# Two PSUM banks for the projections in the whole kernel, and another order of the fp32 matmuls in each block

## Chip, core and metric

One core of a Trainium2 chip runs the whole kernel. The metric is the device time of one execution in microseconds, given as the median of several runs; the profile is one further execution of the same program, taken by the hardware profiler. Its engines are TensorE (PE, matmuls and transpositions; PEld is its weight load), VectorE (DVE), ScalarE (ACT), GpSimd (POOL), and SyncE (SP), which issues most DMAs. Matmul results land in PSUM, which this kernel uses as eight banks of 128 partitions x 512 fp32.

## What is computed

One layer of a hybrid trunk, for 256 prompt tokens and 8 x 16 sample tokens, that is T = 384 columns. All matrices are fp32.

```python
u = rmsnorm(x)                                  # D_MODEL = 2048
proj = u @ w_in                                 # columns: pool | z | xBC | dt | gates
# branch A: windowed means (2, 4, 8, 16) minus self, a map per group of channels
d = win / cnt - p;  a_pool = (d @ pool_w[g]) * pool_scale
# branch B: causal convolution and silu on x, B, C, then a chunked scan with a state
dt = softplus(dt_raw + dt_bias);  cum = cumsum(dt * A)
cb = einsum('btgn,bsgn->btsg', C, B)
y = einsum('btsgr,bsgrp->btgrp', cb * exp(cum_t - cum_s), x * dt)    # within a chunk
y = y + einsum('btgn,bgrpn->btgrp', C, h) * exp(cum)                 # from the state
h = h * exp(last) + einsum('bsgn,bsgr,bsgrp->bgrpn', B, w_end, x * dt)
a_ssd = gated_rmsnorm(y + d_skip * x, z)
m = sigmoid(gA) * (a_pool @ w_pool_proj) + sigmoid(gB) * (a_ssd @ w_ssd_proj)
x = x + rmsnorm(m @ w_out)
x = x + rmsnorm(relu(rmsnorm(x) @ w_up) ** 2 @ w_down)
```

The outputs are x of both groups of requests, and the new pooling, convolution and scan states.

## The kernel before

**A projection.** Most of the work is `out[128, 384] = W.T @ x`, with the tokens as columns. To keep fp32 accuracy in the fp32r format, both sides are split into a high and a low part, and each product is three matmuls (`mm3`, lines 81 to 83: high x high, high x low, low x high). Weights come in units of 128 x 1024, which hold 8 contraction tiles: SP loads a unit (`wfetch`, tag w, three buffers), ACT rounds its high part (line 72), DVE subtracts (line 74, `wl`); the high and low parts have three buffers each. A projection of 2048 inputs is two units ("halves"), 48 matmuls; `w_ssd` has four. Each projection is one PSUM tile `pj_...`, which one DVE instruction (two for the pooling) reads when it is done.

**PSUM.** There are two pools. `psm` has two banks (`mmtile`), `pss` has six (`sstile`), and each new tile of a pool takes its banks in turn, so that its first write waits until the tile that held the bank before has been read. `bank[0]` says which pool `proj` takes. It is `sstile` everywhere but in the loop over blocks, where it is `mmtile`; everything else (transpositions, norms, the scan's tiles, the outputs of w_out and w_down) is in `sstile` throughout.

**Order.** Instructions are recorded in program order with the tiles that they read and write; a scheduler then sets the order on each engine, each of which runs its instructions strictly in that order. `behind` (line 59) ties an instruction behind another; in the blocks, `half` and `lump` use it to chain projections and groups of small matmuls on TensorE as they are written.

**The stages,** with their time in the profile:

1. To some 36 us: x is loaded and split, pj_p0 and pj_p1 (early, in `sstile` by name) and pj_p2 are computed, and the norm of x (`norm_bc`, bc_x, line 109) gives `rstd`.
2. To 190 us: `pool_tile` (line 223) for 16 tiles, four of each window. It reads `pj_p` with rstd into one of two buffers `pbuf` (lines 230 and 231), fills in the state (line 237), forms the window sums `win` (line 246), the difference `d` (lines 249 to 262) and its split `dh`, `dl` (lines 265, 266). `pool_map` (line 269) multiplies four of these with `pool_w` into `pw` tiles.
3. `dt_phase` (line 295): pj_dt, then a chain of some twenty DVE instructions on 64 partitions (lines 303 to 319) that ends in `cum`, the exponentials, `dtw`, and eleven small transpositions `tk` (line 345) to `tok`. Then, to some 470 us, 16 times a gate projection `pj_ga` (read by `gat`, line 290) and a `pj_pp` (read by `ma`, line 363).
4. To some 1300 us: eight blocks (line 646). In each, six projections `pj_x` through the convolution (`conv`), four `pj_z`, most often a `pj_gb`, and the scan for two pairs of heads. The scan's fp32 matmuls stand in two lumps: after the fifth `pj_x` (trB, yT, Y, pp, cb, trx, yi) and after the last `pj_z` (yT, Y, pp, trx, yi). trB and trx are transpositions of B and x (three records for each 128 x 384), yT puts the transposed state term into the two Y tiles and Y adds to it with 64-column tiles (`128*64`), cb is C times B, yi is C times the state with 32-column tiles (`128*32`) into one half of a bank `py`, and pp is the new state of the prompt into the other half. fp32 matmuls other than transpositions show as two records each. After them, `bside` reads trB, `mside` makes `cbm` from cb on DVE (line 525), `final` reads Y and pp, `xside` reads trx and yi, and `eside` forms the decay `E` with exponentials on ACT.
5. To 1780 us: the last gates, `pj_sp` (w_ssd), and w_out with the tokens as rows (`moving`).
6. From 1780 us: x1 = x + norm (line 849), 16 tiles `trm` of three transpositions each (line 859) with their split x1h, x1l (lines 863, 864), the norm of x1 by way of `dg` (line 879) and bc2 (line 881) to r2, then eight rounds of eight `pj_up` (read with r2, line 903) and the products with w_down (`wd`, three banks at a time).

Of the kernel before, what the change touches and what calls it, by code (L numbers as in the profile page):

```python
# [15 lines left out]
T = 384  # L16
# [18 lines left out]
def build(ctx, tc, io):  # L35
# [15 lines left out]
    def mmtile(name):  # L51
        return psm.tile([P, 512], F32, tag="mm", name=name)

    def sstile(name):
        return pss.tile([P, 512], F32, tag="ss", name=name)
# [27 lines left out]
        return te.matmul(out, wl, xh, start=False, stop=last)  # L83

    last = [None]
    bank = [sstile]
    chain = [False]

    def half(o, q, wl_, rhs):
# [276 lines left out]
    with tc.tile_pool(name="phd", bufs=2, reuse_waits="tile") as pd, tc.tile_pool(  # L366
# [46 lines left out]
        def lump(fn):  # L413
            with behind(last[0]):
                last[0] = fn()
# [15 lines left out]
        def t_trB(D):  # L431
            D.tr = sstile(f"trB{D.g}")
            for b in range(3):
                i = te.transpose(D.tr[:, b * P : b * P + P], D.BT[:, b * P : b * P + P], ident)
            return i
# [204 lines left out]
            S.h0 = S.qd * 4  # L640
            return S

        bank[0] = mmtile
        chain[0] = True
        prev = None
        for g in range(G + 1):
            if g == G:
                dside(prev.p[1])
                gate_b()
                state(prev.p[1])  # L650
                gate_b()
                py = sstile("pp_last")
                lump(lambda: t_yT(prev.p[1]))
                lump(lambda: t_Y(prev.p[1]))
                lump(lambda: t_pp(prev.p[1], py))
                final(prev.p[1])
                gate_b()
                gate_b()
                finish(prev)
                break  # L660
            u0 = 49 + g * 10
            D = Pair()
            D.g = g
            D.p = [pair(D, jp) for jp in range(2)]
            D.xs, D.zs = [], []
            D.BT = conv(u0, 32 + g, "BT", 2)
            pload(D.p[0])
            if g:
                dside(prev.p[1])
            D.CT = conv(u0 + 1, 40 + g, "CT", 2)  # L670
            if g:
                state(prev.p[1])
            D.xs.append(conv(u0 + 2, g * 4, "xs", 6))
            cload(D.p[0])
            cside(D)
            D.xs.append(conv(u0 + 3, g * 4 + 1, "xs", 6))
            D.xs.append(conv(u0 + 4, g * 4 + 2, "xs", 6))
            S = D.p[0]
            lump(lambda: t_trB(D))
            bside(D)  # L680
            if g:
                lump(lambda: t_yT(prev.p[1]))
                lump(lambda: t_Y(prev.p[1]))
            S.py = sstile(f"py{S.nm}")
            if g:
                lump(lambda: t_pp(prev.p[1], S.py))
            lump(lambda: t_cb(D))
            lump(lambda: t_trx(S))
            lump(lambda: t_yi(S))
            if g:  # L690
                final(prev.p[1])
            xside(S)
            mside(D)
            D.xs.append(conv(u0 + 5, g * 4 + 3, "xs", 6))
            eside(S, 0)

            def zproj(j):
                ps = proj(in_units(u0 + 6 + j), xg, f"z{g}_{j}")
                z = pd.tile([P, T], F32, tag="zs", name=f"zs{g}_{j}", bufs=7)
                v.tensor_tensor(z, ps, rstd, ALU.mult)  # L700
                s.activation(z, z, AF.Silu)
                D.zs.append(z)

            zproj(0)
            if g:
                finish(prev)
            pload(D.p[1])
            eside(S, 1)
            zproj(1)
            dside(S)  # L710
            zproj(2)
            state(S)
            cload(D.p[1])
            zproj(3)
            S1 = D.p[1]
            lump(lambda: t_yT(S))
            lump(lambda: t_Y(S))
            S1.py = sstile(f"py{S1.nm}")
            lump(lambda: t_pp(S, S1.py))
            lump(lambda: t_trx(S1))  # L720
            lump(lambda: t_yi(S1))
            final(S)
            xside(S1)
            if g < NG:
                gate_b()
            eside(S1, 0)
            eside(S1, 1)
            prev = D
        bank[0] = sstile
        while gates:  # L730
            gate_b()
        chain[0] = False
# [135 lines left out]
    with tc.tile_pool(name="phg", bufs=1, reuse_waits="tile") as pg, tc.tile_pool(  # L868
        name="phg2", bufs=2, reuse_waits="tile"
    ) as pg2:  # L870
        st = pg.tile([P, 3, 4], F32, name="st2")
        for b in range(3):
            for i in range(4):
                q = pg2.tile([P, 512], F32, tag="q3", name=f"q2_{b}_{i}")
                s.activation(q, x1[:, b, blk(i)], AF.Square, accum_out=st[:, b, i : i + 1])
        dg = pg.tile([P, 3, P], F32, name="dg2")
        for b in range(3):
            y = postnorm(pg2, st, b, "n2")
            v.tensor_scalar(dg[:, b, :], ident, y, None, ALU.mult)
        bc = sstile("bc2")  # L880
        te.matmul(bc[:, :T], ones, dg.rearrange("p b t -> p (b t)"), start=True, stop=True)  # L881
        s.copy(r2, bc[:, :T])
        hacc = pg.tile([P, 3, DM], F32, name="hacc")
        gpo = pg.tile([P, DM], F32, name="gpo2")
        gp.dma_start(gpo, io["g_mlp_post"].partition_broadcast(P))
        s.activation(gpo, gpo, AF.Copy, scale=-0.5)
        st3 = pg.tile([P, 3, 4], F32, name="st3")
        pg.tile([P, 96], F32, name="pad_e")
        NC = 8
        for c8 in range(NC):  # L890
            hh = []
            for f8 in range(8):
                f = c8 * 8 + f8
                if f == 0:
                    ps = sstile("pj_up0")[:, :T]
                    half(ps, 0, wload(io["w_up"][0, 0], "up0_0"), xs2)
                    hold[:] = gate
                    half(ps, 1, wload(io["w_up"][0, 1], "up0_1"), xs2)
                else:
                    ps = proj([io["w_up"][f, 0], io["w_up"][f, 1]], xs2, f"up{f}")  # L900
                    hold[:] = [None, None]
                t = pg2.tile([P, T], F32, tag="t", name=f"ht{f}")
                v.scalar_tensor_tensor(out=t, in0=ps, scalar=0.0, in1=r2, op0=ALU.max, op1=ALU.mult)
                s.activation(t, t, AF.Square)
                h = pg2.tile([P, T], F32R, tag=f"hh{f8}", name=f"hh{f}", bufs=1)
                l = pg2.tile([P, T], F32R, tag=f"hl{f8}", name=f"hl{f}", bufs=1)
                s.activation(h, t, AF.Copy)
                v.tensor_tensor(l, t, h.bitcast(F32), ALU.subtract)
                hh.append((h, l))
            for nb in range(4):  # L910
                o = [sstile(f"wd{c8}_{nb}_{b}") for b in range(3)]

                def done(b):
                    dst = hacc[:, b, blk(nb)]
                    if c8 == 0:
                        s.copy(dst, o[b])
                        return
                    v.tensor_tensor(dst, o[b], dst, ALU.add)  # L918
                    if c8 < NC - 1:
                        return  # L920
                    q = pg2.tile([P, 512], F32, tag="q3", name=f"q3_{nb}_{b}")
                    s.activation(q, dst, AF.Square, accum_out=st3[:, b, nb : nb + 1])  # L922
                    if nb < 3:
                        v.tensor_tensor(dst, dst, gpo[:, blk(nb)], ALU.mult)
                        return
                    if b == 0:
                        pg.tile([P, 32], F32, name="pad_z")
                    z3 = pg.tile([P, 512], F32, name=f"z3_{b}")
                    v.tensor_tensor(z3, dst, gpo[:, blk(nb)], ALU.mult)
                    y = postnorm(pg2, st3, b, "n3", doubled=True)  # L930
                    for i in range(4):
                        z = z3 if i == 3 else hacc[:, b, blk(i)]
                        v.scalar_tensor_tensor(  # L933
                            out=z, in0=z, scalar=y, in1=x1[:, b, blk(i)], op0=ALU.mult, op1=ALU.add
                        )
                        sy.dma_start(io["y"][b][:, blk(i)], z)

                moving(
                    o,
                    [(io["w_down"][c8, nb, kp], f"wd{c8}_{nb}_{kp}") for kp in range(4)],  # L940
                    hh,
                    4 if c8 == NC - 1 and nb == 3 else 0,
                    done,
                    pg,
                )
# [116 lines left out]
```

## Time and profile before

| what | us |
|---|---|
| median of 3 runs | 2871.39 (2870.82 to 2871.83) |
| the profiled execution | 2871.82 |
| its span, first to last instruction | 2870.1 |
| TensorE waits behind pj_dt, at tk | 15.1 and 1.2 |
| TensorE waits at bc2, behind the last trm | 10.3 |
| TensorE waits at the first pw | 1.4 |
| mean granted TensorE clock in the span | 0.993 |

How to read it: TensorE is in use for nearly the whole span, while DVE is idle for nearly half of it and ACT for more, so time in which TensorE waits or runs at a lower clock counts in full, and idle time of the others counts only where TensorE waits for them. Matmuls overlap in their records: one of 384 columns is shown with 0.33 us, but the next starts 0.17 us after it; so distances between starts are to be read, not lengths. "PEclk" is the share of full clock that TensorE was granted, in tenths, in each of 40 slices of the span. A row of the time line gives the start and the length in us, engine, line, operation, out<-in tiles, the array's tile (rows*columns) and the operand's shape, the number of records merged, and in brackets the engine's idle time before it with the instruction that ended it.

### The profile page before, as it was taken

Reading aid. Unit: us, or ns where it says so; the run is one execution under the profiler, and the core shown is the slowest. Engines: PE = TensorE matmul, PEld = TensorE weight load, DVE = VectorE, ACT = ScalarE, POOL = GpSimd, SP = SyncE. Lnnn points to the kernel's source line nnn. Section 1 sums busy time; section 2 is a strip of 40 time slices with the busy share of each in tenths; the row PEclk is TensorE's granted clock in tenths of the full one; section 3 lists DMA queues with packets and bytes.
Section 4 is the critical chain, followed back from the end, with each engine's and each line's share of the span. In section 5 each row is a group of like instructions: output and inputs, shape, how many; then the busy total and the mean of one; then the engine's idle time right before and its main releaser. Section 6 shows DMA issues by size and latency. Waiting matters only on the chain. (4 is left out here: it accounts for less than half of the span.)

```text
span 2870.1 us, 39341 instructions
## 1 busy us (share of the span) xinstructions
PE 2824.9 (98%) x15823; PEld 2680.8 (93%) x15823; DVE 1568.9 (55%) x2251; ACT 1095.1 (38%) x1590; POOL 96.5 (3%) x156
## 2 busy tenths in 40 slices
PE   9979999999999999999999999899999999999998
PEld 8979999999999999999999987889898999989897
DVE  7773334677876886877533335434444444444445
ACT  5432224354544554444422234433232333333233
POOL 0000000000100100101000000000000000000000
PEclk9989999999999999999999999999999999999999
DMA  6433445556555655566644453334444343334433
GB/s 208 139 111 124 139 143 192 171 186 211 191 183 208 201 181 202 195 210 210 205 153 150 147 183 117 110 126 130 126 127 130 125 132 125 129 128 126 132 125 125
DMA packets 141654, 448.77 MB, mean 156 GB/s; under 512 B 17200, under 2 KB 40816, under 8 KB 136864
## 3 DMA queue, kind: packets, MB, share of 16 engines
q1 hardware_dynamic: 133152, 410.14, 43.9%
q0 software_dynamic: 8320, 36.13, 3.5%
q8 instruction: 124, 2.03, 0.3%
q14 instruction: 58, 0.48, 0.1%
HBM read 404.48 MB, written 41.72 MB: 155 GB/s over the span
## 5 line engine op out<-in xcount | busy, mean ns | idle before, releaser
L81 PE MATMUL pj_up<-x1h,wh_up 128*128 128x384 f32 x1024 | 343.4, 335 | 0.0
L82 PE MATMUL pj_up<-x1l,wh_up 128*128 128x384 f32 x1024 | 342.7, 335 | 0.0
L83 PE MATMUL pj_up<-x1h,wl_up 128*128 128x384 f32 x1024 | 342.7, 335 | 0.0
L74 DVE TENSOR_TENSOR wl_wd<-w_wd,wh_wd 128x1024 fp32r<-128x1024 f32 x127 | 155.6, 1225 | 262.0 <-ACT wh_wd L72 262.0
L777 PE MATMUL wd<-wl_wd,hh 128*128 128x512 f32 x762 | 296.7, 389 | 0.0
L778 PE MATMUL wd<-wh_wd,hl 128*128 128x512 f32 x762 | 296.6, 389 | 0.0
L776 PE MATMUL wd<-wh_wd,hh 128*128 128x512 f32 x762 | 296.2, 389 | 0.0
L74 DVE TENSOR_TENSOR wl_up<-w_up,wh_up 128x1024 fp32r<-128x1024 f32 x128 | 156.9, 1226 | 208.9 <-ACT wh_up L72 208.9
L72 ACT ACTIVATE wh_wd<-w_wd 128x1024 fp32r<-128x1024 f32 x127 | 135.0, 1063 | 350.4 <-PE wd L778 282.6
L72 ACT ACTIVATE wh_up<-w_up 128x1024 fp32r<-128x1024 f32 x128 | 136.0, 1064 | 336.3 <-PE pj_up L82 275.7
L81 PE MATMUL pj_x<-xgh,wh_x 128*128 128x384 f32 x768 | 257.5, 335 | 0.0
L83 PE MATMUL pj_x<-xgh,wl_x 128*128 128x384 f32 x768 | 256.6, 334 | 0.0
L82 PE MATMUL pj_x<-xgl,wh_x 128*128 128x384 f32 x768 | 256.6, 334 | 0.0
L81 PEld LDWEIGHTS pj_up<-x1h,wh_up 128*128 128x128 f32 x1024 | 192.8, 188 | 0.6 <-issue 0.3
L82 PEld LDWEIGHTS pj_up<-x1l,wh_up 128*128 128x128 f32 x1024 | 192.8, 188 | 0.6 <-issue 0.3
L83 PEld LDWEIGHTS pj_up<-x1h,wl_up 128*128 128x128 f32 x1024 | 192.7, 188 | 0.0
L81 PE MATMUL pj_z<-xgh,wh_z 128*128 128x384 f32 x512 | 171.1, 334 | 0.0
L83 PE MATMUL pj_z<-xgh,wl_z 128*128 128x384 f32 x512 | 171.1, 334 | 0.0
L82 PE MATMUL pj_z<-xgl,wh_z 128*128 128x384 f32 x512 | 171.0, 334 | 0.0
L81 PE MATMUL pj_sp<-abh,wh_sp 128*128 128x384 f32 x512 | 171.0, 334 | 0.0
L82 PE MATMUL pj_sp<-abl,wh_sp 128*128 128x384 f32 x512 | 171.0, 334 | 0.0
L83 PE MATMUL pj_sp<-abh,wl_sp 128*128 128x384 f32 x512 | 171.0, 334 | 0.0
(291 smaller groups left out, 6058.4 us busy)
## 6 DMA issues: line engine op xcount, KB each, us to landing
w_up<-w_up SPq DMA_DIRECT2D x128, 512.0 KB, 3.4
w_wd<-w_down SPq DMA_DIRECT2D x128, 512.0 KB, 3.4
w_x<-w_in SPq DMA_DIRECT2D x96, 512.0 KB, 4.2
w_z<-w_in SPq DMA_DIRECT2D x64, 512.0 KB, 3.5
w_sp<-w_ssd SPq DMA_DIRECT2D x64, 512.0 KB, 3.5
w_ga<-w_in SPq DMA_DIRECT2D x32, 512.0 KB, 3.4
w_pp<-w_pp SPq DMA_DIRECT2D x32, 512.0 KB, 3.4
hs<-ssm SPq DMA_DIRECT2D x16, 1024.0 KB, 6.0
```

The lines of the kernel that those rows point to most:

```text
L72: s.activation(h, w, AF.Copy)
L74: v.tensor_tensor(l, w, h.bitcast(F32), ALU.subtract)
L81: te.matmul(out, wh, xh, start=first, stop=False)
L82: te.matmul(out, wh, xl, start=False, stop=False)
L83: return te.matmul(out, wl, xh, start=False, stop=last)
L776: te.matmul(o[b], mh, wh[:, c], start=k == 0, stop=False)
L777: te.matmul(o[b], mh, wl[:, c], start=False, stop=False)
L778: te.matmul(o[b], ml, wh[:, c], start=False, stop=k == nk - 1)
```

## The change

`bank` starts as `mmtile` and is never set again, so every projection of `proj` is in the two banks of `psm`, in all stages; pj_up0, which is written out by hand, also goes there, while pj_p0 and pj_p1 stay in `sstile`. So in stages 1 to 3, 5 and 6, the six banks hold only the other tiles. In the blocks, the lumps are written in another order. First lump: cb, trB, trx, yT, Y, yi, pp in place of trB, yT, Y, pp, cb, trx, yi, with `mside` right behind cb in place of behind `xside`. Second lump: trx, yT, Y, yi, pp in place of yT, Y, pp, trx, yi. As `py` is now taken last in the first lump, it takes the bank that cb had.

```diff
     last = [None]
-    bank = [sstile]
+    bank = [mmtile]
     chain = [False]
...
-        bank[0] = mmtile
         chain[0] = True
...
             S = D.p[0]
+            lump(lambda: t_cb(D))
+            mside(D)
             lump(lambda: t_trB(D))
             bside(D)
+            lump(lambda: t_trx(S))
             if g:
                 lump(lambda: t_yT(prev.p[1]))
                 lump(lambda: t_Y(prev.p[1]))
             S.py = sstile(f"py{S.nm}")
+            lump(lambda: t_yi(S))
             if g:
                 lump(lambda: t_pp(prev.p[1], S.py))
-            lump(lambda: t_cb(D))
-            lump(lambda: t_trx(S))
-            lump(lambda: t_yi(S))
             if g:
                 final(prev.p[1])
             xside(S)
-            mside(D)
...
             S1 = D.p[1]
+            lump(lambda: t_trx(S1))
             lump(lambda: t_yT(S))
             lump(lambda: t_Y(S))
             S1.py = sstile(f"py{S1.nm}")
+            lump(lambda: t_yi(S1))
             lump(lambda: t_pp(S, S1.py))
-            lump(lambda: t_trx(S1))
-            lump(lambda: t_yi(S1))
             final(S)
...
             prev = D
-        bank[0] = sstile
         while gates:
             gate_b()
...
                 if f == 0:
-                    ps = sstile("pj_up0")[:, :T]
+                    ps = mmtile("pj_up0")[:, :T]
                     half(ps, 0, wload(io["w_up"][0, 0], "up0_0"), xs2)
```

## The prediction

> **What bounds the kernel now.** I read the busy shares on the page first, then the list of TensorE's waits, then the time line around each wait, then around the small fp32 matmuls.
>
> ```profile
> span 2870.1 us, 39341 instructions
> PE 2824.9 (98%) x15823; PEld 2680.8 (93%) x15823; DVE 1568.9 (55%) x2251; ACT 1095.1 (38%) x1590; POOL 96.5 (3%) x156
> PEclk9989999999999999999999999999999999999999
> ```
>
> TensorE sets the time: a 384-column matmul starts every 0.1735 us in the time line, whatever the other engines do. Only three things can change it: a wait of TensorE, the clock it is granted, and what a matmul's start costs its neighbour. The list of waits (engine, line, who ended it, us in total, times, longest) is short:
>
> ```profile
> PE tk L345 <- DVE cum L319: 15.1, 1, 15.1
> PE bc L881 <- DVE dg L879: 10.3, 1, 10.3
> PE trm L859 <- DVE x L849: 2.4, 2, 2.0
> PE pw L81 <- ACT dh L265: 1.4, 1, 1.4
> PE tk L345 <- DVE dtw L333: 1.2, 1, 1.2
> ```
>
> The first, in the time line of TensorE (start us, length us, ... [idle before]):
>
> ```profile
> 195.96 0.34 PE L83 MATMUL pj_dt<-xgh,wl_dt 128*128 128x384 f32 x1
> 211.40 0.58 PE L345 MATMUL tk<-cst,cum 64*128 64x64 f32 x3 [15.10 <-DVE cum L319]
> ...
> 214.24 0.69 PE L81 MATMUL pj_pp<-ah,wh_pp 128*128 128x384 f32 x1
> 214.72 0.52 PE L82 MATMUL pj_pp<-al,wh_pp 128*128 128x384 f32 x1
> ```
>
> After the wait a matmul takes 0.52 instead of 0.34: starts are 0.320 apart, and the granted clock is 0.50 until 220.2. In a block, one of its two lumps of small matmuls:
>
> ```profile
> 723.37 0.49 PE L434 MATMUL trB<-cst,xs 128*128 128x128 f32 x3
> 723.69 0.38 PE L471 MATMUL Y<-cst,yis 128*128 128x128 f32 x2
> 724.00 1.96 PE L479 MATMUL Y<-E,xdt 128*64 128x256 f32 x24
> 725.89 1.16 PE L493 MATMUL py<-Bk,xdw 128*128 128x128 f32 x8
> 726.88 1.04 PE L440 MATMUL cb<-xs,xs 128*128 128x256 f32 x6
> 727.76 0.82 PE L450 MATMUL trx<-cst,xs 128*128 128x128 f32 x6
> 728.51 1.09 PE L458 MATMUL py<-hs,Cm 128*32 128x256 f32 x16
> 729.53 0.44 PE L81 MATMUL pj_x<-xgh,wh_x 128*128 128x384 f32 x1
> ```
>
> No wait is in it, but starts are unevenly spaced: see the third part.
>
> **The change, part by part.** No instruction goes and none is added, except an ACT table load per block from the second on. What moves is the order on each engine, since a projection no longer queues for a bank behind transposes and block tiles.
>
> *1. After dt_phase (gain 18.3).* In the built order the tk transpositions no longer follow pj_dt. TensorE goes on with pj_pp0 and pj_ga1 (48 matmuls each) and 17 of pj_pp1: 113 x 0.1735 = 19.6 us of cover. The DVE chain to cum ended 15.1 us after pj_dt. It now has wl_ga, ma, wl_pp twice, gat and wl_ga between its steps (four splits of 1.23, two of 0.55), and each waits for ACT or TensorE. Laid out with the time line's durations: reciprocal to 202.5, ma 204.7 (end of pj_pp0), six Horner steps to 210.2, gat 213.5 (end of pj_ga1: 212.95), cum at 216.4. TensorE is there at 215.7, so 0.7 us of wait. The dtw transpositions come 14 matmuls later, dtw itself at 218.5: no wait. On SP, the writes of cum and dec now stand behind four weight loads; the next load behind them is needed some 16 us later. Today the place costs 214.24 - 196.13 = 18.1 us, plus 5.96 us at half clock, where 0.32 instead of 0.1735 loses 46%: 2.7. Of these 20.8, tk's own 1.2, two changes of shape at 0.3 (tk to pj_pp: 0.24 for 0.11, then 0.17) and the 0.7 stay. Ends: 19.0 without a wait, 12.6 if cum is 3 us later and the clock falls again (2.7).
>
> *2. From w_out to w_up (gain 11).* pj_up0 now has a bank of its own, so its matmuls stand between the trm transpositions, and bc2 behind all 48 of pj_up0 and 7 of pj_up1. Until 1784.6 nothing changes (x1 sets it). Then TensorE has 36 transpositions and 14 matmuls, at half clock to 1790.3 as today, and ends trm15 at 1794.2 instead of 1792.3. ACT and DVE are some 0.7 us later, so dg comes at 1803.2 instead of 1802.5. TensorE reaches bc2 at 1801.5 and waits 1.7. I count no loss of clock for it (the 2.0 us wait at 1782.5 did lose it, but came right after two others; a loss would be 1.6, inside the ends). Today: 1784.6 to 1803.5, and 2.2 lost at half clock, 21.1 in all. After: bc2 ends at 1804.1, less 55 x 0.1735 = 9.5 of projection already done: 10.0. r2 comes at 1805, and pj_up0's bank is free at 1806, before pj_up2 wants it at 1811. Ends: 8 and 12.
>
> *3. The third pool tile (loss 6.1).* pj_p0 and pj_p1 stay among the six banks, but pj_p2, pj_p3 and pj_p4 now share two, so pj_p4 waits for pj_p2's reader, which waits for rstd. rstd is there at 44.80, and pj_p4 started at 44.61:
>
> ```profile
> 44.83 0.43 DVE L230 TENSOR_TENSOR pbuf<-pj_p,rstd 128x256 f32<-128x256 f32 x1
> ...
> 51.09 1.30 DVE L246 TENSOR_TENSOR win<-pbuf 128x518 f32<-128x518 f32 x2
> ```
>
> The buffers pbuf are two, so pj_p2 is read after win, d and dh of tile 0. win is no longer behind the second wl_pw, so the row at 51.09 moves to 47.0; d0 is then done at 49.4, dh0 at 49.9, dl0 at 50.5, pj_p2's second reader at 50.8. TensorE does three pw matmuls in the gap (0.5) and starts pj_p4 at 50.9: 6.3 - 0.5 = 5.7 lost. Its idle stretch of 5.4 us lies between waits of 2.0 and 10.3 that both lost clock; 6 us at half clock after one cost 2.7, 3.4 us would cost 1.6: I take 2.0. In return the pw wait of 1.4 (1.65 with its restart) goes. Ends: 3.5 and 9. [...]
>
> *4. The lumps (gain 3.2).* Starts in the lump, ns: trx to trx 109, trx to yi 203, then 200 for 176; last yi to pj 309, then 281 for 173; Y to Y 103, Y to pp 202, then 214 for 112; pp to cb 111; pp to pj (last block) 31 and 259. So a change from whole columns into yi costs 118, out of yi 241, out of Y 201, and pp to pj nothing. Today each lump pays 201 + 118 + 241 = 560. After: Y to yi, unknown; yi to pp, between 201 and 241; pp to pj 0. For Y to yi the nearest row is the entry into yi, 118, from which I take it: 560 - 118 - 221, about 215 ns, by 15 lumps. Ends: 5 (Y to yi free) and -3.5 (pp to pj pays again).
>
> py now takes cb's bank, so yi waits until cbm has read cb. In the built order cbm stands third on DVE after the lump starts; behind cbuf, wl_z and one cacc, which end at 726.09 in this lump, it ends at 726.7, and yi is due 4.05 us after the start, at 727.4. Slack 0.7. The extra table loads (1.28) fall on ACT: wh_z's second half ends near 735.8 and its DVE half near 737.9, wanted at 742.
>
> *5. Elsewhere two banks cost nothing.* The reader of a projection ends at most 4.8 us after it (gb tail, 1387.8), 4.1 us or more before the second next one starts.
>
> Sum: 18.3 + 11 + 3.2 - 6.1 = 26.4. The span becomes 2870.1 - 26.4 = 2843.7; the profiled execution took 2871.82 with 1.7 around its span, and the median shown is 2871.39. From that: 2845.0.
>
> **Rivals.** *Slower: cbm holds the lumps.* If cbm stays where DVE has it today, behind the readers of Y and trx:
>
> ```profile
> 732.11 0.68 DVE L525 TENSOR_TENSOR cbm<-cb,cst 128x512 f32<-128x512 f32 x1
> ```
>
> it ends 9.4 us after the lump's start, yi waits 5.3 in each of seven lumps, and each wait costs about 2 of clock: 51 us, 2896. It turns the sign once yi waits 3.8 (26.4 / 7). Against: the built order puts cbm ahead. 4%.
>
> *The cover of tk is too thin:* the steps put into DVE's chain wait one after another, cum is 3 us later, the clock falls: 2850.7. For: each waits for TensorE or ACT. 13%.
>
> *Given back:* bc2's wait only moves to pj_up2, whose bank needs r2, and a third of tk's gain goes: 2862. Against: 5 us of room. 6%.
>
> *pj_p4 doesn't wait,* because it isn't bound to pj_p2's bank: 2845.0 - 7.7 = 2837.3. 6%.
>
> *Two banks starve projections everywhere.* If each of the 132 projections that are new on them waited 0.6 (the smallest wait at a start, bc_x), 79 us: 2924. Against: the blocks already run theirs on these two banks, and a projection's first matmul there starts 173 to 176 ns after the last. 3%. [...]
>
> **How the numbers follow.** The forecast has 68%, its own range 2839 to 2852. The range for 8 in 10 takes in pj_p4 without a wait and the thin cover: 2836 to 2857. A measurement of this kernel tells some 0.2% (5.7 us) from no change. Faster: forecast, thin cover, no wait, nearly all of given back: 92%. Same: 2%. Slower: cbm, starvation: 6%.
>
> **What would show it.** In TensorE's waits: no 15.1 at tk and no 10.3 at bc, under 2 us each; a new wait of 5 to 6 us at pw0 or pj_p4, near 45 us, with a low clock digit there; lumps of 6.1 and 4.9 us instead of 6.34 and 5.14; no wait at py. I am wrong if yi waits for cbm, if tk waits over 3 us, or if any projection after 60 us waits for its bank.

## The result and the profile after

The changed kernel takes 2847.01 us (median of six runs, 2845.91 to 2847.74) where the kernel before, run beside it, takes 2871.11 (2869.47 to 2872.54). The ratio is 0.9916, 95% interval 0.9903 to 0.9929: 24.1 us faster. The profiled execution has a span of 2845.6 us against 2870.1, 24.5 us less. The page, first lines and the row of granted clock:

```profile
span 2845.6 us, 39445 instructions
...
PE 2818.9 (99%) x15823; PEld 2676.3 (94%) x15823; DVE 1574.4 (55%) x2251; ACT 1096.4 (39%) x1592; POOL 97.0 (3%) x156
...
PEclk9999999999999999999999999999999999999999
```

TensorE issues the same 15823 matmuls; its busy time falls by 6.0 us, because fewer of them run at half clock (between the kernel's start and its tail, three stretches of 20.5, 6.8 and 10.2 us in before, two of 6.8 here) and the lumps are shorter. The slice that had an 8 in the row of clock (143 to 215 us) has a 9. Its waits (engine, line, who ended it, us in total, times, longest):

```profile
PE pw L81 <- ACT dh L265: 5.2, 1, 5.2
...
PE trm L857 <- DVE x L847: 2.4, 2, 2.0
PE bc L879 <- DVE dg L877: 1.3, 1, 1.3
...
PE su L590 <- DMA xst<-x_scr: 0.8, 1, 0.8
...
PE tk L345 <- DVE cum L319: 0.5, 1, 0.5
```

The 15.1 at tk and the 10.3 at bc are gone. The 5.2 at pw is new and was forecast. The 0.8 at su is new and was not. The time line of TensorE around tk:

```profile
202.17 0.33 PE L83 MATMUL pj_dt<-xgh,wl_dt 128*128 128x384 f32 x1
202.35 0.33 PE L81 MATMUL pj_pp<-ah,wh_pp 128*128 128x384 f32 x1
...
222.61 0.40 PE L345 MATMUL tk<-cst,cum 64*128 64x64 f32 x3 [0.51 <-DVE cum L319]
```

20 us of projections now stand between pj_dt and tk, at full clock (0.33 us a matmul, where before had 0.52 behind its wait). VectorE's chain is stretched as laid out, with weight splits in it:

```profile
219.68 0.54 DVE L290 TENSOR_TENSOR gat<-pj_ga,rstd 128x384 f32<-128x384 f32 x1
220.15 0.40 DVE L318 TENSOR_SCALAR dta<-dt,nA 64x384 f32<-64x384 f32 x1
220.47 1.21 DVE L74 TENSOR_TENSOR wl_ga<-w_ga,wh_ga 128x1024 fp32r<-128x1024 f32 x1
221.61 0.94 DVE L319 TENSOR_TENSOR_SCAN cum<-cst,dta 64x384 f32<-64x384 f32 x1
```

The third pool tile, TensorE and then VectorE:

```profile
45.27 0.34 PE L83 MATMUL pj_p<-xgh,wl_p 128*128 128x384 f32 x1
50.81 1.01 PE L81 MATMUL pw<-dh,wh_pw 128*128 128x384 f32 x2 [5.21 <-ACT dh L265]
51.62 0.52 PE L82 MATMUL pw<-dl,wh_pw 128*128 128x384 f32 x1
51.94 0.52 PE L81 MATMUL pj_p<-xgh,wh_p 128*128 128x384 f32 x1
```

```profile
51.36 0.28 DVE L231 TENSOR_TENSOR pbuf<-pj_p,rstd 128x128 f32<-128x128 f32 x1
```

The list of waits names ScalarE's dh, for three matmuls of pw stood first in line. These rows alone do not show that the bank is the cause: pj_p4 starts at 51.94, which is one step at half clock (0.32 us) behind the last of the three. They do fit it, for the second reader of pj_p2, whose bank pj_p4 takes, ends only at 51.36 + 0.28 = 51.64. The test is x_early1 below, which gives pj_p2 another bank. The lump that the prediction showed, now:

```profile
710.02 1.04 PE L440 MATMUL cb<-xs,xs 128*128 128x256 f32 x6
710.89 0.49 PE L434 MATMUL trB<-cst,xs 128*128 128x128 f32 x3
711.22 0.82 PE L450 MATMUL trx<-cst,xs 128*128 128x128 f32 x6
711.87 0.38 PE L471 MATMUL Y<-cst,yis 128*128 128x128 f32 x2
712.19 1.96 PE L479 MATMUL Y<-E,xdt 128*64 128x256 f32 x24
714.07 1.09 PE L458 MATMUL py<-hs,Cm 128*32 128x256 f32 x16
715.09 1.16 PE L493 MATMUL py<-Bk,xdw 128*128 128x128 f32 x8
```

The next projection's first matmul starts at 716.01. From the projection's matmul ahead of the lump to the one behind it, as the prediction counted, it is 6.16 us in place of 6.34, and 4.96 in place of 5.14 in the other lump of a block. From the first lump of one block to that of the next it is 104.78 us in place of 105.15. Two lumps lie in that distance, so one is worth 0.187 us on average.

Where the 24.5 us are is read from the start of the same matmul in both traces, after minus before, at points between the places: +0.8 us at pj_p3, +6.2 at pj_dt, -12.75 at the third pj_ga, -14.55 at the first trm, -24.5 at pj_up2 and at the end. So the pool tile cost 5.4, tk gave 19.0, the blocks 1.8, w_out to w_up 10.0, and 0.8 was lost in the first 36 us, among waits for the first inputs that vary from run to run (pj_p's for xgh come to 1.2 us in this trace, to none in the list of before, and to 0.2 to 1.4 in those of the experiments).

### The profile page after: what moved, and what is told of

Read it like the earlier page. It is cut to its first block, busy times and chain, and to the rows that moved or that the text cites. A ratio compares the mean times of both kernels' runs of the same rounds, so it can differ in the third digit from the quotient of the medians.

```text
span 2845.6 us, 39445 instructions
## 1 busy us (share of the span) xinstructions
PE 2818.9 (99%) x15823; PEld 2676.3 (94%) x15823; DVE 1574.4 (55%) x2251; ACT 1096.4 (39%) x1592; POOL 97.0 (3%) x156
## 4 chain that ended last, share of the span: by engine, by line
PE 96%; DVE 2%; ACT 1%; DMA 1%; issue 0%; SPq 0%; DVEq 0%; ACTq 0%
PE pj_up L83 6%; PE pj_up L81 6%; PE pj_up L82 6%; PE wd L775 6%; PE wd L776 6%; PE wd L774 6%; PE pj_x L81 5%; PE pj_x L83 5%; PE pj_x L82 5%; PE pj_sp L82 3%; PE pj_z L81 3%; PE pj_z L82 3%; PE pj_sp L83 3%; PE pj_z L83 3%; PE pj_sp L81 3%; PE pj_pp L83 2%
## 5 line engine op out<-in xcount | busy, mean ns | idle before, releaser
L775 PEld LDWEIGHTS wd<-wl_wd,hh 128*128 128x128 f32 x762 | 143.0, 188 | 29.8 <-DVE wl_wd L74 0.3
```

Of the source, the lines that this page charges most:

```text
L775: te.matmul(o[b], mh, wl[:, c], start=False, stop=False)
```

## Experiments

Each is timed against the kernel before on the same chip. The medians of the kernel before lie between 2870.94 and 2871.47 us on the chips used, so times of different runs can be compared to about half a microsecond. The diffs are against the changed kernel unless another is named.

**The two halves of the change.** x_banks is the kernel before with only the banks changed, x_lumps the kernel before with only the order in the lumps changed.

```diff
 x_banks (against before)
-    bank = [sstile]
+    bank = [mmtile]
...
-        bank[0] = mmtile
...
-        bank[0] = sstile
...
-                    ps = sstile("pj_up0")[:, :T]
+                    ps = mmtile("pj_up0")[:, :T]
```

> Only the banks are changed: every projection has the two banks of its own, the lumps keep the order of before. Theory (four places that add up: tk +19.0, w_up +10.0, pool tile -5.4, lumps +2.7): the lumps' 2.7 us are missing, 2847.0 + 2.7 = 2849.7 us, with 0.5 us of wait at tk, 1 to 2 at bc2, 5 at the first pw, and lumps of 6.34 and 5.14 us. Rival (the new order of the lumps is what carries the gain, the long stalls only change their place): above 2860 us.

> Only the order in the lumps is changed: the projections outside the blocks go round the six banks as before. Theory: 2.7 us faster than before, 2868.4 us, with lumps of 6.16 and 4.96 us in place of 6.34 and 5.14, and with the waits of 15.1 us at tk and 10.3 at bc2 as in before. Rival (the lumps differ only because the blocks stand at another time in the changed kernel, or the order brings a wait for cbm in its own time): 2871 us or more, lumps of 6.3 and 5.1 or a wait at py.

Measured: x_banks 2847.65 us (2846.13 to 2849.45), ratio 0.9917 (0.9901 to 0.9932). x_lumps 2869.64 us (2868.46 to 2871.09) beside 2871.38, ratio 0.9993 (0.9984 to 1.0002). The banks carry nearly all of it. The lumps have the forecast lengths in x_lumps (6.16 and 4.96) and the old ones in x_banks (6.34 and 5.14), and yet they are worth 1.7 us, not 15 x 0.187 = 2.8. The list of waits of x_lumps says why:

```profile
PE tk L345 <- DVE cum L319: 15.1, 1, 15.1
PE bc L881 <- DVE dg L879: 9.9, 1, 9.9
...
PE su L590 <- DMA xst<-x_scr: 0.8, 1, 0.8
```

The two long waits are as before; the wait of su is there too, and it is not in x_banks nor in before. So it belongs to the order of the lumps. From the matmul ahead of this su to the one behind it, start to start, it is 2.16 us in place of 1.13, so it costs 1.0 us. 2.8 - 1.0 = 1.8; the trace of x_lumps is 1.79 us shorter than that of before from the first pj_x to the first trm, and the runs show 1.7. The interval of x_lumps reaches 1.0002, so its time alone would not prove a gain; the lump lengths do. x_banks came out only 0.6 us above the changed kernel, and not 1.7, and its forecast of 2849.7 was missed. Its trace shows where: from the first pj_x to the first trm it is 1.81 us longer than the changed kernel's, as the lumps ask, but it reaches the first pj_x 0.87 us sooner and needs 0.81 us less from the first trm to the first product with w_down. The edit touches neither of these two stretches, so that the two spans are equal (2845.6 us) is chance.

**The two long places one at a time.** x_tk_six puts the projections from pj_ga0 through dt to the last pj_pp back on the six banks, x_up_six those of w_ssd and w_up behind the blocks.

```diff
 x_tk_six
+        bank[0] = sstile
         sg = gate_a(0)
         pool_map(3)
...
             gp.dma_start(ma_scr[n], m)
+        bank[0] = mmtile
...
 x_up_six
     main.close()
+    bank[0] = sstile
...
-                    ps = mmtile("pj_up0")[:, :T]
+                    ps = sstile("pj_up0")[:, :T]
```

> The changed kernel, with only the projections from pj_ga0 through dt to the last pj_pp back on the six banks. Theory (the place around tk was worth 19.0 us by itself): 2847.0 + 19.0 = 2866.0 us, the wait of 15.1 us at tk and the half clock from about 206 to 226 us are back. Rival (TensorE gets ahead for another reason, such as the earlier start of the weight loads): under 2855 us.

> The changed kernel, with the projections after the blocks (pj_sp and pj_up, pj_up0 too) on the six banks. Theory (the place from w_out to w_up was worth 10.0 us by itself): 2847.0 + 10.0 = 2857.0 us, with a wait of 10 us at bc2 and trm's transpositions in one piece. Rival (bc2's wait is set by ScalarE's squares and comes whatever the banks are, so that only the matmuls before it were regained elsewhere): 2847 to 2850 us.

Measured: x_tk_six 2863.93 us (2862.58 to 2868.57), x_up_six 2858.73 (2857.30 to 2859.58): 16.9 and 11.7 us over the changed kernel by the medians, 19.5 and 9.9 by the spans. The eight runs of x_tk_six spread over 6.0 us, and the profiled one is among the longest three, so its figure is the least certain. From x_tk_six's waits:

```profile
PE tk L345 <- DVE cum L319: 15.1, 1, 15.1
PE pw L81 <- ACT dh L265: 5.2, 1, 5.2
```

and from x_up_six's:

```profile
PE bc L880 <- DVE dg L878: 9.7, 1, 9.7
```

Each wait comes back alone, with a half clock that begins in it (206.5 to 227.0 us in the one, 1780.4 to 1790.6 in the other). Both rivals fall.

**What the lumps save.** x_pp_yi exchanges yi and pp, and keeps everything else of the new order.

```diff
             S.py = sstile(f"py{S.nm}")
-            lump(lambda: t_yi(S))
             if g:
                 lump(lambda: t_pp(prev.p[1], S.py))
+            lump(lambda: t_yi(S))
...
-            lump(lambda: t_yi(S1))
             lump(lambda: t_pp(S, S1.py))
+            lump(lambda: t_yi(S1))
```

> The changed kernel, with pp and yi exchanged in the lumps: Y, pp, yi, and the transpositions together as before. Theory (what the new order saves is a change of the form of the tiles: Y to yi and yi to pp cost 359 ns together, where Y to pp, pp to yi and yi to the projection cost 560): lumps of 6.34 and 5.14 us again, 15 x 0.18 = 2.7 us more, but without su's wait for xst where yi stands last as in the kernel before: 2848.8 to 2849.7 us. Rival (the gain comes from bringing the transpositions together and cb to the front): lumps of 6.16 and 4.96 us, 2847.0 us.

Measured: 2849.07 us (2848.11 to 2849.69), with lumps of 6.34 and 5.14 us again. The end of a lump, time line of TensorE:

```profile
711.94 1.96 PE L479 MATMUL Y<-E,xdt 128*64 128x256 f32 x24
713.82 1.16 PE L493 MATMUL py<-Bk,xdw 128*128 128x128 f32 x8
714.91 1.09 PE L458 MATMUL py<-hs,Cm 128*32 128x256 f32 x16
...
715.93 0.45 PE L81 MATMUL pj_x<-xgh,wh_x 128*128 128x384 f32 x1
```

From Y's first start to the projection it is 3.99 us here and 716.01 - 712.19 = 3.82 in the changed kernel, for the same matmuls. The form of the tiles is in the fifth column of words: 128*64, 128*128, 128*32, 128*128 here; 128*64, 128*32, 128*128, 128*128 there. One change of form fewer is the whole gain in the lumps; that the transpositions come together does not shorten them. One part of the expectation missed: su's wait for xst stays (0.7 us), so it does not come from yi's place. What x_pp_yi shares with the changed kernel is that trx stands ahead of Y.

**Which banks, and how many.** x_early1 puts pj_p2 back among the six banks, so that pj_p3 and pj_p4 have the two. x_psm3 gives the projections three banks and the rest five.

```diff
 x_early1
+    bank[0] = sstile
     early += [proj(in_units(1 + k), xg, f"p{k}") for k in (2,)]
+    bank[0] = mmtile
...
 x_psm3
-    psm = ctx.enter_context(tc.tile_pool(name="psm", bufs=2, space=PSUM))
-    pss = ctx.enter_context(tc.tile_pool(name="pss", bufs=6, space=PSUM))
+    psm = ctx.enter_context(tc.tile_pool(name="psm", bufs=3, space=PSUM))
+    pss = ctx.enter_context(tc.tile_pool(name="pss", bufs=5, space=PSUM))
```

> The changed kernel, with pj_p2 alone put back among the six banks, so that pj_p3 and pj_p4 have the two and pj_p4 waits for nobody. Theory (the wait of 5.2 us at the first pw and the half clock behind it are pj_p4's wait for the bank of pj_p2): the 5.4 us come back, 2841.6 us, with the wait of some 1.4 us at pw that before has. Rival (the two banks only hand the wait on: pj_p5 or pj_p6 now waits for the readers of pj_p3 and pj_p4, which stand behind rstd too): 2845 to 2847 us, with a new wait at pj_p between 55 and 80 us.

> The changed kernel with three banks for the projections and five for the rest. Theory: pj_p4 finds a free bank, which gives back 5.4 us; but a block's first lump holds seven tiles, so the second Y takes cb's bank and py that of trB: Y waits for cbm, which ended 713.33 - 710.02 = 3.3 us after the lump's start, where its transposition came 1.9 to 2.0 us after it: some 1.4 us in each of seven blocks, 10 us, so 2847.0 - 5.4 + 10 = 2851.6 us, and up to 2866 us if each wait halves the clock for a time. Rival (six banks are more than the lumps need): 2841.6 us, no wait in the lumps.

Measured: x_early1 2840.87 us (2840.48 to 2841.37), ratio 0.9892 (0.9879 to 0.9906); x_psm3 2851.26 (2850.72 to 2852.18). In x_early1 pw waits 1.4 us as in before, pj_p4 starts at 44.94, no later projection waits for a bank, and no half clock is left near there: the stall was one bank's and is gone. In x_psm3 it is gone too, but each of seven blocks has this in its lump:

```profile
707.16 0.82 PE L450 MATMUL trx<-cst,xs 128*128 128x128 f32 x6
707.81 0.27 PE L471 MATMUL Y<-cst,yis 128*128 128x128 f32 x1
709.34 0.33 PE L471 MATMUL Y<-cst,yis 128*128 128x128 f32 x1 [1.25 <-DVE cbm L525]
```

The second Y has cb's bank and waits for cbm. The second Y starts 1.53 us after the first where it starts 0.11 after it in the changed kernel; seven times 1.42 are the 10 us that were expected. Two banks and six is the division that fits these lumps; the prediction's rival in which cbm holds the lumps is this mechanism, one bank away.

**The late transfer of xst, and a cover that was forgotten.** In the last block only one projection stands between the second lump and su. Counted from the start of that lump, VectorE ends xhl at 7.15 us and the transfers to xst start at 9.22 in before; in the changed kernel it is 8.11 and 10.18, since VectorE now has two steps of E, with a wait in them, ahead of xhl where it had one. From before, and from x_early1:

```profile
1296.48 0.28 DVE L564 TENSOR_SCALAR E<-cbc,tok 128x128 f32<-128x128 f32 x1
1296.73 0.43 DVE L547 TENSOR_TENSOR xhl<-xdw,xhl 128x256 fp32r<-128x256 f32 x1
...
1275.30 1.17 DVE L566 TENSOR_SCALAR E<-cbc,tok 128x128 f32<-128x128 f32 x2
1276.39 0.41 DVE L549 TENSOR_TENSOR xhl<-xdw,xhl 128x256 fp32r<-128x256 f32 x1
```

x_best is x_early1 with a gate projection in the last block; x_best2 takes that projection from block 0 in place of the end of the stage.

```diff
 x_best (against x_early1)
-            if g < NG:
+            if g < NG or g == G - 1:
                 gate_b()
...
 x_best2 (against x_early1)
-            if g < NG:
+            if 0 < g < NG or g == G - 1:
                 gate_b()
```

> The changed kernel with pj_p2 among the six banks (as in x_early1, 2840.9 us), and with one gate projection, taken from the end of the stage, put between the last pair's lump and its su. Theory (the new order of the lumps leaves xst of the last pair 0.8 us late, because only one projection stands between its lump and su where the other pairs have two or more): the wait of su for xst goes, which with its restart is 0.95 us: 2839.9 us. Rival (the transfer is late for another reason, such as the queue it goes through): 2840.9 us, su waits 0.8 us as in x_early1.

> As x_best, but the gate projection between the last pair's lump and its su is taken from block 0 and not from the end of the stage, so that eight projections stand behind the last pp again, as in x_early1. Theory (x_best lost its time because one projection fewer covered the way of the last block's output through its scratch to pj_sp, which cost 3.8 us of wait and 6.8 us at half clock): no wait at pj_sp and none of su for xst, 0.95 us under x_early1: 2839.9 us. Rival (a gate in the last block delays that block's side work whatever it is taken from): pj_sp waits again, 2845 us or more.

Measured: x_best 2846.65 us (2844.91 to 2847.31), 5.8 us slower than x_early1, where neither theory nor rival had put it. su's wait went as expected (pj_sp starts 1.0 us earlier), but the list of waits has a new first line:

```profile
PE pj_sp L81 <- ACT abh L746: 3.8, 2, 2.2
```

The last block's outputs go through a_scr and come back as abh while the gate projections at the end of the stage run; with seven in place of eight of them behind the last pp, pj_sp overtakes the reload, waits 3.8 us and runs 6.8 us at half clock. x_best2 leaves eight there: 2839.13 us (2838.32 to 2840.09), ratio 0.9889 (0.9872 to 0.9905), no wait at pj_sp and none at su; in its trace the blocks end 1.0 us earlier than in x_early1.

**Is it the clock or ScalarE behind x1?** x_fill is x_best2 with eleven matmuls that feed nothing in the wait before the third transpositions of trm. To make room for them, the transpositions of the first six tiles are also taken in another order, all first ones, then all second ones, then all third ones.

```diff
+    trs = [sstile(f"trm{k}") for k in range(6)]
+    lt = None
+    for b in range(3):
+        if b == 2:
+            fl = mmtile("fill")
+            with behind(lt):
+                for _ in range(11):
+                    lt = te.matmul(fl[:, :T], onesr, ms_[0][0], start=True, stop=True)
+        for k in range(6):
+            with behind(lt):
+                lt = te.transpose(trs[k][:, b * P : b * P + P], x1[:, b, k * P : k * P + P], ident)
     for k in range(KD):
-        tr = sstile(f"trm{k}")
-        for b in range(3):
+        tr = trs[k] if k < 6 else sstile(f"trm{k}")
+        for b in range(3 if k >= 6 else 0):
```

> x_best2 with eleven matmuls of 384 columns, whose result nobody reads, in TensorE's wait of 2.0 us between the trm transpositions (and the first six tiles' transpositions issued third by third). Theory (the clock falls for the idle time, but what sets the end of this stage is ScalarE, which goes from the x1h splits into the squares for bc2 and had waited for the transpositions 1.6 us in all): no half clock after trm, bc2's wait grows from 1.3 to 2 to 3.5 us, and the time falls by 0 to 1.6 us: 2838.3 to 2839.9 us. Rival (the half clock itself costs its 3.3 us on the path): bc2's wait stays near 1.3 us, 2836.6 us. Or the clock falls all the same: then the wait isn't what brings it down.

Measured: 2837.88 us (2836.61 to 2839.76), ratio 0.9884 (0.9869 to 0.9898). The time line of TensorE:

```profile
1760.35 0.98 PE L866 MATMUL trm<-cst,x 128*128 128x128 f32 x7 [1.74 <-DVE hm L837]
1761.09 2.18 PE L863 MATMUL fill<-mh,onesr 128*128 128x384 f32 x11
1763.11 0.84 PE L866 MATMUL trm<-cst,x 128*128 128x128 f32 x6
...
1766.50 0.55 PE L870 MATMUL trm<-cst,x 128*128 128x128 f32 x3 [1.83 <-DVE x1l L875]
```

In this trace the clock holds at 1.0 through the whole stage (0.999 in the mean of the span, 0.998 in x_best2). So the drop did not come with the stage's work alone: here the same work and eleven matmuls more, with the idle time laid otherwise, ran without it. As the edit both fills a wait and moves others, it does not show which wait goes with the drop. The gain is about 1.3 us by the medians, with ranges that overlap, and it does not come the way either theory said: bc2 has no wait left, because in the built order it now stands behind 20 matmuls of pj_up1 in place of 8, and two waits of 1.7 and 1.8 us stand earlier in their stead.

What a half clock costs here is read better from the kept traces, from the first trm to the first product with w_down. That stretch takes 82.56 us in x_early1, with 6.8 us of half clock, 80.56 in x_best2, with 3.4, and 79.79 in x_fill, with none. x_early1 and x_best2 have the same instructions there, and the second 3.4 us cost 2.0, which is no less than the 1.6 us by which a step of 0.320 in place of 0.1735 delays 3.4 us of matmuls. Between x_best2 and x_fill, 3.4 us of half clock go for a gain of 0.8 only, but there bc2's place and the waits changed as well. That speaks against the theory that ScalarE sets the end of this stage whatever the clock is. How the last 0.8 us divide stays open. Each of these figures is from one execution.

## Why the prediction was right, and which terms were off

It said 2845.0 us; 2847.01 was measured, inside the forecast's own range. All four mechanisms are in the trace and came back or went one at a time. That the sum came out within 2 us is in part luck: the terms were off by +0.7, -1.0, -1.4 and +0.7 us, which partly cancel, and no term stood for the 0.8 us lost at the start.

| place | predicted | trace | by the run that undoes it or does it alone |
|---|---|---|---|
| tk | 18.3 | 19.0 | 16.9 (x_tk_six) |
| w_out to w_up | 11 | 10.0 | 11.7 (x_up_six) |
| lumps, with su's new wait | 3.2 | 1.8 | 1.7 (x_lumps) |
| third pool tile | -6.1 | -5.4 | -6.1 (x_early1) |
| sum | 26.4 | 25.4, less 0.8 at the start | 24.2 |

1. *tk.* Laid out to 0.1 us: cum was forecast to end at 216.4, in the times of before; it ends at 221.61 + 0.94 = 222.55, which less the 6.2 us by which the stage starts later is 216.3. The wait is 0.5 where 0.7 was forecast. Of the old cost 2.5 us were to stay; counted from start to start around the two groups of tk, 1.7 stayed, and that is the 0.7 by which the term was too small. The rival of the thin cover did not come.

2. *w_out to w_up.* The order and the wait of bc2 came as forecast (1.3 us for 1.7), but 1.4 us later: bc2 starts at 1790.06, which is 1804.6 in the times of before, not 1803.2. The step that was off is "at half clock to 1790.3 as today". The half clock lasted from 1771.35 to 1778.17, 6.8 us as in before, but it began 2.4 us later against the work, and so ended at 1792.7 in the times of before. It did not keep its place, and it came in few lengths: in these traces, by the granted clock, every such stretch between the kernel's start and its tail is 3.4, 6.8, 10.2 or 20.5 us long (20.5, 6.8 and 10.2 in before, 6.8 twice in the changed kernel). Behind x1 it was 6.8 us in x_early1 and 3.4 us in x_best2, which has the same instructions there, and in which this stage ends 2.0 us sooner. So a term with half clock in it can differ by some 2 us from one execution to the next, an estimate from these two traces that no better reading of one trace removes, and the measured 10.0 holds for that execution.

3. *Third pool tile.* With the 0.8 us of late start taken off, dh0 was forecast to be done at 49.9 and is at 49.9, the second reader of pj_p2 at 50.8 and is at 50.8. The order of events came as laid out, and the two terms are a little too large. Counted from start to start against a step of 0.1735, the wait loses 5.4 us where 5.7 were charged, and the half clock behind it 1.75 where 2.0 were charged. The half clock lasted 6.8 us (47.62 to 54.45), but it began 3.2 us before the wait ended, and in a wait it costs nothing. With the 1.7 us that went with the old wait at pw, the place cost 5.4 in all. All five traces with this wait have a half clock, for 3.4 us in three of them and 6.8 in two. The 2.0 was the author's choice between 2.7 for 6 us at half clock and 1.6 for 3.4 us; the trace of before has no stretch as short as 3.4, so nothing had shown that end when it was taken.

4. *Lumps.* The step "Y to yi: I take it from the entry into yi" held: Y to yi costs 124 ns where 118 was taken, yi to pp 235 where 221 was taken, pp to the projection nothing. That leaves 201 + 118 + 241 - 359 = 201 ns, and 187 were measured, 2.8 us in 15 lumps where 3.2 was forecast. (As the prediction wrote it, 560 - 118 - 221 is 221 ns and not 215, which is 0.1 us in all.) What was missed is a price elsewhere. The prediction followed cbm and two table loads, but not xhl, which came later on VectorE, behind two steps of E, and made the last su start 1.0 us later. Moving transpositions forward moves all their readers, and these were not followed to the end.

5. *Two banks elsewhere.* No projection waits for a bank after the third pool tile, and the clock holds 1.0 from 54.45 to 1771.35 us. The rival of starvation fell, and x_psm3 shows that a third bank would have been the wrong cure.

## What to carry to other kernels

Give the stream that fills the bottleneck engine buffers of its own, so that its order is not tied to side work that waits for a slow chain; then look for the one place where that stream's readers are late (here the start, before rstd) and leave it in the larger pool. Count the independent work that stands between a producer's end and its use before moving any of it: one projection of 8.3 us taken from the end of the stage (x_best) cost 5.8 us net. Where matmuls of several tile forms stand together, put them in the order with the fewest changes of form (one fewer was worth 187 ns a lump here).

## What the runs showed of the hardware

- A change of form between small fp32 matmuls had a price that differed with the two forms. By the starts in the lumps of the kernel before and the changed kernel it was: from 64 columns to 128 about 201 ns, from 64 to 32 124, from 128 to 32 118, from 32 back to 128 235 to 241. From pp, whole columns, to the projection there was none: the next two starts follow after 31 and 257 ns, where unchanged ones take 112 and 174.
- In x_psm3 a wait of some 1.24 us in each of seven lumps (8.7 in all) was followed by no half clock (1.0 from 11.6 to 1776.3 us), and in x_fill waits of 1.74 and 1.83 us, with matmuls between them, were not either. A wait of 2.0 us right after two shorter ones (0.35 to 0.73 us) was followed by a half clock of 3.4 or 6.8 us in each of the eleven other traces.
- With eleven matmuls that feed nothing, and the transpositions in another order, the clock stayed at 1.0 through that place in the one trace of x_fill.
